# Attention scores of a hybrid decoder: the low-part query product over all 128 rows, and the causal mask added in the bias

## The chip, the cores and the metric

One Trainium2 chip, one of its cores. The metric is the device time of one launch in microseconds (us); lower is better. Five engines work side by side: TensorE (PE, with its weight loads PEld), VectorE (DVE), ScalarE (ACT), GpSimd (POOL) and SyncE (SP), whose queue issues nearly all DMAs. Each engine executes its own instructions in the order in which the program lists them and waits at each for the semaphores that it needs.

## The reference

A trunk of two layers on 1024 tokens of 1024 channels, all in float32. Layer 0 is a gated convolution (Conformer) with a feed-forward network and an embedding gate; layer 1 is forgetting attention with 16 heads of 64 channels, again with a feed-forward network and a gate. The part that matters here:

```
q = (hn @ w_q).reshape(B, S, N_HEADS, HEAD_DIM) * (HEAD_DIM ** -0.5)
...
s = jnp.einsum("bqhd,bkhd->bhqk", q_blk, k,
bias = c_blk[:, :, :, None] - c_bhs[:, :, None, :]
causal = k_pos[None, :] <= q_pos[:, None]
s = jnp.where(causal, s + bias, NEG_BIG)
pr = jax.nn.softmax(s, axis=-1)
return jnp.einsum("bhqk,bkhd->bqhd", pr.astype(v.dtype), v)
```

`c` is the running sum of the log forget gates, one number per head and token.

## The kernel before, in words

**Split operands.** TensorE multiplies float32r operands, so each float32 operand is kept as two parts, a high one `h` (a cast, `split`, L107) and a low one `l` (the subtraction, L108); a product is three products of parts (`mm3`, L130). Weights come panel by panel (`panel`, L110): a DMA from SP (L113) into a tile `raw` (L112, two buffers in the whole program, tag "raw"), the norm's gain multiplied in on GpSimd (L118), then the split. Squares and their sum for a norm's statistics are in `rstd` (squares L166, sum `acc` L187 and L189, its own buffer).

**Attention** (`attention`, L458) goes over 8 pairs of heads. A pair has 8 units: 4 groups of 256 queries (u = 3, 2, 1, 0; in the last pair 0, 1, 2, 3) times two heads (e = 0, 1), 64 units in all. `scores` (L683) makes a unit's probabilities for two blocks of 128 queries: GpSimd writes the bias c(query) - c(key) into a slot of the tile `pr` (L696), TensorE adds up the score in pieces of up to 512 keys, DVE adds bias and score and takes the row's extreme (L714), ACT exponentiates and sums (L720), DVE inverts the sum (L721), GpSimd scales (L722). A score piece is two products: L705 over 128 rows (the high query part times both key parts) and L706 over the 64 rows of this head (the low query part `ql` times the high key part). In the last piece of a block a third product adds the causal mask: a bf16 identity times a bf16 mask of 128 columns (L710). There are 192 pieces, 3 per unit on average, and 128 blocks. `values` (L725) transposes the probabilities on TensorE (L770), splits them, and multiplies by V (L740); it runs one unit behind `scores`.

**Fills.** Between the units stand products that do not depend on them: the queries and keys of the next pair (`project_qk`, psq and psk), the values of the next four heads (`project_v`, psv). In the last two pairs, when there is nothing left to project, the output product (`out_product`, L558, ps_wo) of the first five pairs stands there; its weights come through `panel` too. A scheduler puts the program in order by its own estimates; the pools of tiles and their numbers of buffers enter into it. Every tile that is not yet released makes the engine that wants it wait.

Of the kernel before, what the change touches and what calls it, by code (L numbers as in the profile page):

```python
# [10 lines left out]
F32 = mybir.dt.float32  # L11
F32R = mybir.dt.float32r
BF16 = mybir.dt.bfloat16
# [5 lines left out]
P = 128  # L19
# [15 lines left out]
# columns of the packed per-channel vectors: name -> (offset, number of 128-row tiles)  # L35
# [24 lines left out]
class K:  # L60
    def __init__(self, ctx, tc, a):
# [3 lines left out]
        self.wp = ctx.enter_context(tc.tile_pool(name="wp", bufs=3))  # L65
# [13 lines left out]
        # the sigmoid's table holds what the first stage needs  # L79
# [9 lines left out]

    def slot(self, shape, dt, name):  # L90
        return self.big.tile(shape, dt, name=name, tag="big")

    def tmp(self, name, dt=F32, cols=HB):
        return self.tp.tile([P, cols], dt, name=name, tag="t")
# [15 lines left out]
    def panel(self, src, kt, name, gain=None, k0=0, width=P, sub=None):  # L110
        nc = self.nc
        raw = self.wp.tile([P, kt * width], F32, name=f"raw_{name}", tag="raw", bufs=2)  # L112
# [31 lines left out]
    def bcast(self, col, name):  # L144
        """[128 tokens, 4] -> PSUM [128, 512]: the tokens' value in every partition."""
# [25 lines left out]
    def rstd(self, xs, name, late=0, ahead=URGENT):  # L171
        """xs(k) -> [128, 512]; 1/sqrt(mean of squares + eps): SBUF [128 tokens, 4], PSUM [128, 512]."""
# [4 lines left out]
        def reduce(x, first, last):  # L177
            # the sum over the partitions, one token per partition
# [7 lines left out]
        acc = self.tp.tile([P, HB], F32, name=f"acc_{name}", tag="acc", bufs=1)  # L186
# [25 lines left out]
    def operand(self, hT, h, gain, name, pool=None):  # L212
        """float32r parts of h * gain; the norm's factor per token is applied to the products."""
# [31 lines left out]
    def ple_proj(self, l, ahead):  # L245
        """p[l] @ w_proj[l], transposed, kept in DRAM."""
# [3 lines left out]
        for k in range(KP):  # L250
            with self.tc.high_priority(offset=ahead()):
                raw = self.wp.tile([P, T], F32, name=f"raw_p{l}{k}", tag="raw", bufs=2)
# [17 lines left out]
    def glu(self, hT, u, cs, halves, x, s):  # L270
        """first pointwise product and gate, into u [128, 30 + T] per channel tile."""
# [46 lines left out]
            # two sums in PSUM, so that a step reads SBUF once and leaves GpSimd its port  # L318
# [13 lines left out]
    def ln_silu(self, y, h):  # L332
        nc = self.nc
        yk = lambda k: y[:, k, :]
        acc = self.tp.tile([P, HB], F32, name=f"acc_m{h}", tag="acc", bufs=1)
# [80 lines left out]
    def first(self, hT):  # L416
        """convolution layer, first FFN and embedding gate."""
        nc, tc = self.nc, self.tc
        self.subs = (nc.gpsimd, None)
        with ExitStack() as c1:  # L420
            self.psum_pools(c1, 0, 4)
# [36 lines left out]
    def attention(self, hT):  # L458
# [6 lines left out]
        with ExitStack() as c2:  # L465
            self.at = self.pool(c2, "at", 2)
# [6 lines left out]
            mask = self.cp.tile([P, P], BF16, name="mask")  # L473
# [5 lines left out]
            idb = self.cp.tile([P, P], BF16, name="idb")  # L479
            nc.vector.tensor_copy(idb, self.ident)  # L480
            self.mask, self.idb = mask, idb
# [53 lines left out]
        c3 = ExitStack()  # L535
        self.psum_pools(c3, 2)
# [11 lines left out]
    def load_o(self, od, p):  # L548
        """head pair p of the output product's operand."""
        if self.xo is None:  # L550
            self.xo = [self.xpair("xo", h) for h in range(NH)]
        raw = self.wp.tile([P, T], F32, name=f"raw_o{p}", tag="raw", bufs=2)
# [5 lines left out]
    def out_product(self, k0, k1, halves=(0, 1)):  # L558
# [10 lines left out]
    def gates(self, cd):  # L569
        """cumulative log forget gates: DRAM [head, token] and SBUF [token, block, head]."""  # L570
        nc = self.nc
        g = self.at.tile([P, 2, T], F32, name="gate", tag="pr")
        u, e, lt, x = (g[:, 0, i * P : (i + 1) * P] for i in range(4))
        z = self.zf.rearrange("p b n -> p (b n)")
        # log_sigmoid(z) = min(z, 0) - log1p(exp(-|z|)), log1p with its rounding put back
# [11 lines left out]
        # sums within a block of 128 tokens, and over the blocks before it  # L587
# [10 lines left out]
        rows = g[0:N, 1, :]  # L598
        for h in range(NH):
# [3 lines left out]
            nc.scalar.copy(rows[:, h * HB : (h + 1) * HB], st[0:N, :])  # L603
# [12 lines left out]
    def project_v(self, g, dst):  # L616
        """values of the four heads of group g, in pieces."""
# [31 lines left out]
    def project_qk(self, p, dst):  # L649
        """queries and keys of the two heads of pair p, in pieces."""  # L650
# [217 lines left out]
```

## Time and profile before

| | us |
|---|---|
| device time, median of 3 runs | 2696.07 (2693.39 to 2699.38) |
| span of the profiled execution (first to last instruction) | 2692.4 |
| PE busy | 2628.9 |
| DVE / ACT / POOL busy | 1532.9 / 1003.4 / 592.8 |

The profiled execution has no time of its own on the page beside its span; the median of the runs lies 3.7 us above that span. Within the span the first layer ends near 1190 us, attention goes from there to 1859 us, and the second layer's feed-forward network, gate and last norm take the rest. A PE instruction's "busy" time is longer than its distance to the next one, since matmuls overlap; the distance from start to start is what a product costs in a row of products.

### The profile page before, as it was taken

To read this page: it belongs to the slowest core of one execution; us is meant where nothing else is said; L and a number is where in the kernel's file an instruction comes from. 1 tells how busy PE (TensorE), PEld (TensorE's weight loads), DVE (VectorE), ACT (ScalarE), POOL (GpSimd) and SP (SyncE) were. 2 spreads that over 40 slices of the span, in tenths; PEclk is the share of its full clock that TensorE was granted. 3 is DMA by queue.
4 is the path that set the end of the run, shared out by engine and by line. 5 is a ranking of instruction groups with operands and counts; after the bars stand their busy time and mean duration, and the time that the engine had idled before them with its cause. 6 is when DMAs were issued, how large, how long until landed. Compare 5 with 4: busy or idle time off the path is not lost.

```text
span 2692.4 us, 31503 instructions
## 1 busy us (share of the span) xinstructions
PE 2628.9 (98%) x12184; PEld 2110.3 (78%) x12184; DVE 1532.9 (57%) x2536; ACT 1003.4 (37%) x1608; POOL 592.8 (22%) x525
## 2 busy tenths in 40 slices
PE   7997999999999999999999999999999999999998
PEld 6885778888888888888777787778888888888886
DVE  7999999734444335566666666766323323223466
ACT  5245433333333224334555554654312202113242
POOL 3464544444000000013444443340000000000000
PEclk9998999999999999999999999999999999999998
DMA  3124222222222222231111111321111111111123
GB/s 128 47 73 170 68 89 94 93 95 93 96 87 94 94 94 98 94 123 56 57 39 54 40 56 62 102 83 62 47 47 48 47 47 48 47 47 51 48 98 133
DMA packets 63973, 205.26 MB, mean 76 GB/s; under 512 B 7360, under 2 KB 12096, under 8 KB 63312
## 3 DMA queue, kind: packets, MB, share of 16 engines
q1 hardware_dynamic: 62672, 199.06, 21.9%
q10 hardware_dynamic: 1152, 4.19, 0.4%
q8 instruction: 96, 1.57, 0.2%
q14 instruction: 53, 0.43, 0.1%
HBM read 182.71 MB, written 20.51 MB: 75 GB/s over the span
## 4 chain that ended last, share of the span: by engine, by line
PE 89%; DVE 6%; issue 2%; POOL 1%; ACT 1%; DMA 1%; POOLq 0%; DVEq 0%; SPq 0%; ACTq 0%
PE ps_fb L130 27%; PE ps_fa L130 25%; PE ps_gt L130 5%; PE psv L130 4%; PE psk L130 3%; PE psq L130 3%; PE ps_wo L130 3%; PE pg L130 3%; PE pa L130 3%; PE po L740 3%; PE s L706 3%; DVE ya L324 2%; PE t L770 2%; PE ps_pw L130 2%; PE s L705 1%
## 5 line engine op out<-in xcount | busy, mean ns | idle before, releaser
L324 DVE SCALAR_TENSOR_TENSOR ya<-u,wdw,ya 128x512 f32<-128x512 f32 x420 | 284.8, 748 | 0.0
L107 ACT CAST wh_fb<-raw_fb 128x1024 fp32r<-128x1024 f32 x96 | 100.6, 1051 | 429.2 <-PE ps_fb L130 306.9
L376 DVE SCALAR_TENSOR_TENSOR fa<-ps_fa,bs_f 128x512 f32<-128x512 f32 x128 | 87.8, 690 | 272.0 <-PE ps_fa L130 269.2
L197 POOL TENSOR_TENSOR r_g<-ms_g,mhalf 128x4 f32<-128x4 f32 x4 | 5.3, 1322 | 1071.3 <-DVE ms_g L195 1071.3
L107 ACT CAST wh_fa<-raw_fa 128x1024 fp32r<-128x1024 f32 x96 | 100.8, 1050 | 348.1 <-PE ps_fa L130 166.8
L130 PE MATMUL ps_fa<-f10xh,wl_fa 128*128 128x512 f32 x512 | 202.7, 396 | 0.0
L130 PE MATMUL ps_fa<-f10xl,wh_fa 128*128 128x512 f32 x512 | 202.5, 396 | 0.0
L130 PE MATMUL ps_fa<-f10xh,wh_fa 128*128 128x512 f32 x512 | 202.5, 396 | 0.0
L382 DVE TENSOR_TENSOR hTb<-ps_fb,hTb 128x512 f32<-128x512 f32 x64 | 44.3, 692 | 246.1 <-PE ps_fb L130 246.1
L108 DVE TENSOR_TENSOR pt<-t,pt 128x512 fp32r<-128x512 f32 (+1 forms) x160 | 99.8, 634 | 90.2 <-ACT pt L107 89.8
L382 DVE TENSOR_TENSOR hT<-ps_fb,hT 128x512 f32<-128x512 f32 x64 | 44.0, 690 | 172.0 <-PE ps_fb L130 171.9
L378 ACT ACTIVATE fa<-fa 128x512 f32<-128x512 f32 x128 | 80.4, 630 | 156.2 <-DVE fa L376 156.1
L722 POOL TENSOR_SCALAR pr<-pr,sm 128x896 f32<-128x896 f32 (+7 forms) x128 | 98.0, 768 | 165.3 <-DVE sm L721 164.2
L107 ACT CAST pt<-t 128x512 fp32r<-128x512 f32 (+1 forms) x160 | 85.1, 542 | 125.6 <-PE t L770 115.7
L714 DVE CUSTOM_DVE_ANT_0 pr<-s,pr 128x512 f32<-128x512 f32 (+2 forms) x192 | 103.2, 552 | 47.9 <-POOL pr L696 20.2
L696 POOL TENSOR_SCALAR pr<-cb,ctok 128x896 f32<-128x896 f32 (+7 forms) x128 | 101.0, 796 | 94.2 <-PE t L770 64.0
L720 ACT ACTIVATE pr<-pr,sm 128x896 f32<-128x896 f32 (+7 forms) x128 | 99.3, 776 | 57.4 <-DVE sm L719 37.3
L740 PE MATMUL po<-pt,V 128*128 128x256 f32 x640 | 115.6, 301 | 1.9 <-ACT pt L107 1.9
L130 PEld LDWEIGHTS ps_fa<-f10xl,wh_fa 128*128 128x128 f32 x512 | 96.3, 188 | 23.1
L130 PEld LDWEIGHTS ps_fa<-f10xh,wl_fa 128*128 128x128 f32 x512 | 96.3, 188 | 23.1
L130 PEld LDWEIGHTS ps_fa<-f10xh,wh_fa 128*128 128x128 f32 x512 | 96.3, 188 | 23.1
L108 POOL TENSOR_TENSOR wl_fa<-raw_fa,wh_fa 128x1024 fp32r<-128x1024 f32 x32 | 80.1, 2504 | 96.8 <-ACT wh_fa L107 96.8
(357 smaller groups left out, 7431.4 us busy)
## 6 DMA issues: line engine op xcount, KB each, us to landing
raw_fa<-in_wf SPq DMA_DIRECT2D x96, 512.0 KB, 3.3
raw_fb<-in_wf SPq DMA_DIRECT2D x96, 512.0 KB, 3.3
raw_gt<-in_wgate SPq DMA_DIRECT2D x24, 512.0 KB, 3.4
proj<-pj SPq DMA_DIRECT2D x32, 256.0 KB, 2.4
raw_pw<-in_wpw SPq DMA_DIRECT2D x16, 512.0 KB, 3.4
lpj<-proj SPq DMA_DIRECT2D x32, 256.0 KB, 3.3
cb<-cd SPq DMA_DIRECT2D x16, 512.0 KB, 3.9
raw_wo<-in_wo SPq DMA_DIRECT2D x16, 320.0 KB, 2.8
```

The lines of the kernel that those rows point to most:

```text
L107: copy(h, src)
L108: sub.tensor_tensor(l, src, h.bitcast(F32), ALU.subtract)
L130: self.nc.tensor.matmul(ps, p[:, k, :], q[:, k, :], start=(start and k == k0 and n == 0), stop=(stop and k == kt - 1 and n == 2),)
L324: nc.vector.scalar_tensor_tensor(d, s(j), w(j), o, ALU.mult, ALU.add)
L376: nc.vector.scalar_tensor_tensor(t, ps, 0.0, s[h][1], ALU.max, ALU.mult)
L382: nc.vector.tensor_tensor(hT[h][:, j, :], ps, hT[h][:, j, :], ALU.add)
L696: nc.gpsimd.tensor_scalar(z, cb[:, 0:W], -1.0, self.ctok[:, i, n : n + 1], ALU.mult, ALU.add)
L706: nc.tensor.matmul(ps[:, 0:cols], ql[r, q], qk[r, 2 + e, kk], start=False, stop=not last)
L714: nc.vector.tensor_tensor_reduce(zz, ps[:, 0 : hi - lo], zz, -1.0, 3.0e38, ALU.add, ALU.min, sm[:, m : m + 1])
L720: nc.scalar.activation(z, z, AF.Exp, bias=sm[:, 0:1], scale=-1.0, accum_out=sm[:, 2:3])
L722: nc.gpsimd.tensor_scalar(z, z, sm[:, 3:4], 1.0, ALU.mult, ALU.mult)
L740: nc.tensor.matmul(po, V[:, j, n % 4, :], pt[:, q, c : c + 256], start=(j == 0 and q == 0), stop=(jp == u and jj == 1 and q == 1),)
```

## The change

The low query part goes into one of two fixed tiles with a plane for each head; the other head's 64 rows are zero, written once (four GpSimd memsets of 64x1024). The low product then runs over 128 rows with the same key operand as L705. The mask product is gone; GpSimd adds a float32 mask of 128x128 to the last 128 columns of each block's bias. The rows of `c` go to DRAM with their sign turned, so that the bias is one addition. `pr` is split into two tags of its own sizes. The tiles that this needs come out of the working pools, which now belong to a stage each: in attention `raw` has 1 buffer (before 2) and the ring of `tmp` has 3 (before 4), the statistics' `acc` comes from that ring, and the output product's panels in attention use the slots of `cb` (the broadcast rows of c, two buffers).

```diff
+    def work_pools(self, ctx, n, raw=2, t=4):
+        self.wp, self.raws = self.pool(ctx, f"wp{n}", 3), raw
+        self.tt = self.pool(ctx, f"tt{n}", t)
...
-        raw = self.wp.tile([P, kt * width], F32, name=f"raw_{name}", tag="raw", bufs=2)
+        if pool is None:
+            raw = self.wp.tile([P, kt * width], F32, name=f"raw_{name}", tag="raw", bufs=self.raws)
+        else:
+            raw = pool.tile([P, kt * width], F32, name=f"raw_{name}", tag=tag)
...
-        acc = self.tp.tile([P, HB], F32, name=f"acc_{name}", tag="acc", bufs=1)
+        acc = self.tmp(f"acc_{name}")
...
+            self.work_pools(c2, 1, 1, 3)
             self.at = self.pool(c2, "at", 2)
...
+            self.qls = [self.at.tile([P, 2, T], F32R, name=f"ql{i}", tag=f"ql{i}", bufs=1) for i in range(2)]
+            for ql in self.qls:
+                for e in range(2):
+                    nc.gpsimd.memset(ql[(1 - e) * HD : (2 - e) * HD, e, :].bitcast(F32), 0.0)
...
-                for _ in self.out_product(0, KSPLIT, (h,)):
+                for _ in self.out_product(0, KSPLIT, (h,), self.at):
...
-            w = self.panel(self.a["wo"][j][:, k0 * P : k1 * P], k1 - k0, f"wo{k0}{j}{halves[0]}")
+            w = self.panel(self.a["wo"][j][:, k0 * P : k1 * P], k1 - k0, f"wo{k0}{j}{halves[0]}", pool=pool, tag="cb")
...
-            nc.scalar.copy(rows[:, h * HB : (h + 1) * HB], st[0:N, :])
+            nc.scalar.mul(rows[:, h * HB : (h + 1) * HB], st[0:N, :], -1.0)
...
-        pr = self.at.tile([P, 2, T], F32, name=f"pr{n}{u}", tag="pr")
+        pr = [self.at.tile([P, T - (1 - b) * P], F32, name=f"pr{n}{u}{b}", tag=f"pr{b}") for b in range(2)]
...
-            nc.gpsimd.tensor_scalar(z, cb[:, 0:W], -1.0, self.ctok[:, i, n : n + 1], ALU.mult, ALU.add)
+            nc.gpsimd.tensor_scalar(z, cb[:, 0:W], self.ctok[:, i, n : n + 1], None, ALU.add)
+            nc.gpsimd.tensor_tensor(z[:, W - P : W], z[:, W - P : W], self.mask, ALU.add)
...
-                    ps[:, 0:cols], ql[r, q], qk[r, 2 + e, kk], start=False, stop=not last
-                )
-                if last:
-                    nc.tensor.matmul(
-                        ps[:, W - P - lo : W - lo], self.idb, self.mask, start=False, stop=True
-                    )
+                    ps[:, 0:cols], ql[:, e, q], qk[:, 2 + e, kk], start=False, stop=True
+                )
```

Line numbers of the changed kernel differ: bias L709, mask addition L710, products L718 and L719, scaling L731, output product's panels L120, memsets of `ql` L493.

**The order, SP, from the end of the embedding gate into attention, before.** lpj are the gate's loads (256 KB each), raw_wv the three panels of the first values' weights, raw_q and raw_k the first query and key panels, hd the store of the residual (2 MB each).

```order
L394 DMA lpj_7871<-proj_1600 128x512
L113 DMA raw_wv_8269<-in_wv 128x816
L394 DMA lpj_7903<-proj_1600 128x512
L394 DMA lpj_7941<-proj_1600 128x512
L113 DMA raw_wv_8276<-in_wv 128x816
L394 DMA lpj_7973<-proj_1600 128x512
L394 DMA lpj_8011<-proj_1600 128x512
L113 DMA raw_wv_8283<-in_wv 128x544
L394 DMA lpj_8043<-proj_1600 128x512
L394 DMA lpj_8081<-proj_1600 128x512
L113 DMA raw_q_8554<-in_wq 128x1024
L394 DMA lpj_8113<-proj_1600 128x512
```

The same queue in the changed kernel:

```order
L401 DMA lpj_8084<-proj_1603 128x512
L401 DMA lpj_8116<-proj_1603 128x512
L120 DMA raw_wv_8284<-in_wv 128x816
L470 DMA hd<-hT_87 128x4096
L470 DMA hd<-hT_92 128x4096
L120 DMA raw_wv_8291<-in_wv 128x816
L120 DMA raw_wv_8298<-in_wv 128x544
L120 DMA raw_q_8569<-in_wq 128x1024
L120 DMA raw_k_8642<-in_wk 128x1024
```

All three panels moved behind the gate's last load, and two of them behind the two stores; each panel from the second on waits until DVE has split the one before it out of the single buffer. On DVE the split of the second panel now stands behind all 14 additions of the statistics' sums.

**The order, PE, the first output product, before** (t and po are transposes and value products of a unit, s its scores):

```order
L770 MATMUL t_13542<-ident,pr_13389 128x128 x3
L705 MATMUL s_13637<-qk_12586 128x512
L706 MATMUL s_13637<-qk_12586,ql_12587 128x512
L710 LDWEIGHTS idb
L710 MATMUL s_13637<-mask,idb 128x128
L130 MATMUL ps_wo_14381<-xoh_13614,wh_wo_14377 128x512
L130 MATMUL ps_wo_14381<-xol_13615,wh_wo_14377 128x512
```

and in the changed kernel:

```order
L749 MATMUL po_14290<-pt_14283,V_11777 128x256 x3
L718 MATMUL s_14300<-qk_13282 128x512
L719 MATMUL s_14300<-qk_13282,ql_8160 128x512
L137 MATMUL ps_wo_14453<-xoh_13674,wh_wo_14449 128x512
L137 MATMUL ps_wo_14453<-xol_13675,wh_wo_14449 128x512
```

Before, 509 of the 640 value products stand ahead of the first output product, now 608; in both kernels 480 stand ahead of the last projection psk. The first panel's slot is that of the `cb` of the last pair, free after the bias of the last unit but one. The mask products are gone between L705/L706 and what follows.

**The order, POOL, the first units in the changed kernel** (before, the four biases, one panel's multiplication and four scalings in a row, no additions):

```order
L709 TENSOR_SCALAR pr_8715<-cb_8711,ctok 128x896
L709 TENSOR_SCALAR pr_8716<-cb_8711,ctok 128x1024
L709 TENSOR_SCALAR pr_8816<-cb_8713,ctok 128x896
L709 TENSOR_SCALAR pr_8817<-cb_8713,ctok 128x1024
L125 TENSOR_TENSOR raw_q_9273<-raw_q_9273,vec 128x1024
L710 TENSOR_TENSOR pr_8715<-pr_8715,mask 128x128
L710 TENSOR_TENSOR pr_8716<-pr_8716,mask 128x128
L710 TENSOR_TENSOR pr_8816<-pr_8816,mask 128x128
L710 TENSOR_TENSOR pr_8817<-pr_8817,mask 128x128
L731 TENSOR_SCALAR pr_8715<-pr_8715,sm_8719 128x896
L731 TENSOR_SCALAR pr_8716<-pr_8716,sm_8734 128x1024
L125 TENSOR_TENSOR raw_k_9447<-raw_k_9447,vec 128x1024
```

A panel's multiplication now stands ahead of the mask additions and another between the scalings; what waits for its DMA there holds back what is behind it.

## Rows read from the trace of the kernel before

**Rows 1.** The page, part 1 (busy time, share) and part 4 (the chain).
```profile
PE 2628.9 (98%) x12184; PEld 2110.3 (78%) x12184; DVE 1532.9 (57%) x2536; ACT 1003.4 (37%) x1608; POOL 592.8 (22%) x525
...
PE 89%; DVE 6%; issue 2%; POOL 1%; ACT 1%; DMA 1%; POOLq 0%; DVEq 0%; SPq 0%; ACTq 0%
```

**Rows 2.** Busy time by stretch: PE, PEld, DVE, ACT, POOL, then PEclk, DMA share, GB/s.
```profile
1366.00:1507.00 141.00, 140.46 (x826) 110.96 (x825) 89.55 (x240) 78.45 (x162) 65.63 (x87) 1.00 0.13 46
...
1859.00:2579.00 720.00, 720.00 (x3104) 580.84 (x3103) 232.14 (x291) 166.57 (x229) 2.04 (x2) 1.00 0.14 48
```

**Rows 3.** Timeline of PE at 1397 us: start, length, line, product.
```profile
1397.41 0.28 PE L130 MATMUL psv<-wl_wv,atxh 128*128 128x256 f32 x1
1397.53 0.40 PE L705 MATMUL s<-qk 128*128 128x512 f32 x1
1397.86 0.49 PE L706 MATMUL s<-qk,ql 64*128 64x512 f32 x1
1398.28 0.23 PE L710 MATMUL s<-mask,idb 128*128 128x128 bf16 x1
1398.32 0.36 PE L130 MATMUL psv<-wh_wv,atxl 128*128 128x256 f32 x1
1398.52 0.40 PE L705 MATMUL s<-qk 128*128 128x512 f32 x1
1398.85 0.50 PE L706 MATMUL s<-qk,ql 64*128 64x512 f32 x1
1399.28 0.39 PE L130 MATMUL psv<-wh_wv,atxh 128*128 128x256 f32 x1
1399.51 0.28 PE L130 MATMUL psv<-wl_wv,atxh 128*128 128x256 f32 x1
```

**Rows 4.** PEld groups, 1225 to 1825 us: count | busy, mean ns | idle before.
```profile
L706 PEld LDWEIGHTS s<-qk,ql 64*128 64x128 f32 x192 | 35.4, 184 | 42.9 <-issue 36.1
```

**Rows 5.** Low product L706 up to 1699 us: ns min/median/max, first and last start.
```profile
L706 PE MATMUL s<-qk,ql x155: 379/491/502, 1245.4 to 1692.8; 64*128 64x512 f32 x80, 64*128 64x256 f32 x49, 64*128 64x384 f32 x26
```

**Rows 6.** Groups of POOL, whole program, shapes kept apart.
```profile
L316 POOL TENSOR_TENSOR y<-y,cm 128x512 f32<-128x512 f32 x30 | 42.0, 1400 | 5.2 <-ACT cm L314 3.5
...
L118 POOL TENSOR_TENSOR raw_q<-raw_q,vec 128x1024 f32<-128x1024 f32 x8 | 16.0, 1994 | 18.5 <-DMA raw_q<-in_wq 18.5
...
L696 POOL TENSOR_SCALAR pr<-cb,ctok 128x128 f32<-128x128 f32 x16 | 6.0, 372 | 3.6 <-PE t L770 2.7 <-POOL pt L772 0.4
```

**Rows 7.** The DMA queue of SP around the end of the embedding gate.
```profile
1167.06 0.33 SPq L113 DMA_DIRECT2D raw_wv<-in_wv  x1
...
1189.92 0.32 SPq L462 DMA_DIRECT2D hd<-hT  x1
...
1192.97 0.32 SPq L462 DMA_DIRECT2D hd<-hT  x1
```

**Rows 8.** The chain of waits from 1183 to 1260 us: start, length, what.
```profile
1189.44 5.78 PE psv L130 x44
...
1221.24 0.47 PE psq L130 x2
```

**Rows 9.** Timeline of DVE: the statistics' sums at 1199 us.
```profile
1199.74 3.99 DVE L189 TENSOR_TENSOR acc_at<-acc_at,sq_at 128x512 f32<-128x512 f32 x4
```

**Rows 10.** DMA issues by line: count, KB each, median us from issue to landing.
```profile
hd<-hT SPq DMA_DIRECT2D x2, 2048.0 KB, 9.1
...
raw_wv<-in_wv SPq DMA_DIRECT2D x2, 408.0 KB, 3.2
```

**Rows 11.** Last key product and all output products: count, ns, first and last start.
```profile
L130 PE MATMUL psk<-atxh,wl_k x128: 392/394/502, 1233.3 to 1698.7; 128*128 128x512 f32 x128
...
L130 PE MATMUL ps_wo<-xoh,wl_wo x128: 392/394/496, 1718.6 to 1858.5; 128*128 128x512 f32 x128
```

**Rows 12.** Busy time by stretch (columns as in rows 2), behind the last key product.
```profile
1707.00:1710.00 3.00, 1.80 (x14) 1.62 (x14) 2.90 (x7) 2.95 (x7) 2.19 (x2) 1.00 0.46 161
1710.00:1718.00 8.00, 7.57 (x27) 4.95 (x27) 7.33 (x21) 4.87 (x10) 2.47 (x4) 0.61 0.32 107
```

More of the change, by code (lines that the diff above doesn't have):

```diff
@@ L64, in __init__ @@
         self.cp = ctx.enter_context(tc.tile_pool(name="cp", bufs=1))
-        self.wp = ctx.enter_context(tc.tile_pool(name="wp", bufs=3))
         self.tp = ctx.enter_context(tc.tile_pool(name="tp", bufs=4))
@@ L93, in tmp @@
     def tmp(self, name, dt=F32, cols=HB):
-        return self.tp.tile([P, cols], dt, name=name, tag="t")
+        return self.tt.tile([P, cols], dt, name=name, tag="t")
     def psum_pools(self, ctx, n, mm=6):
@@ L108, in split, with panel @@
         sub.tensor_tensor(l, src, h.bitcast(F32), ALU.subtract)
-    def panel(self, src, kt, name, gain=None, k0=0, width=P, sub=None):
+    def panel(self, src, kt, name, gain=None, k0=0, width=P, sub=None, pool=None, tag=None):
         nc = self.nc
-        raw = self.wp.tile([P, kt * width], F32, name=f"raw_{name}", tag="raw", bufs=2)
+        if pool is None:
+            raw = self.wp.tile([P, kt * width], F32, name=f"raw_{name}", tag="raw", bufs=self.raws)
+        else:
+            raw = pool.tile([P, kt * width], F32, name=f"raw_{name}", tag=tag)
         nc.sync.dma_start(raw, src)
@@ L251, in ple_proj @@
             with self.tc.high_priority(offset=ahead()):
-                raw = self.wp.tile([P, T], F32, name=f"raw_p{l}{k}", tag="raw", bufs=2)
+                raw = self.wp.tile([P, T], F32, name=f"raw_p{l}{k}", tag="raw", bufs=self.raws)
                 nc.sync.dma_start(raw, self.a["pT"][l, :, k * T : (k + 1) * T])
@@ L334, in ln_silu @@
         yk = lambda k: y[:, k, :]
-        acc = self.tp.tile([P, HB], F32, name=f"acc_m{h}", tag="acc", bufs=1)
+        acc = self.tmp(f"acc_m{h}")
         nc.vector.tensor_tensor(acc, yk(0), yk(1), ALU.add)
@@ L420, in first @@
         with ExitStack() as c1:
+            self.work_pools(c1, 0)
             self.psum_pools(c1, 0, 4)
@@ L472, in attention @@
             self.sqp, self.sqt = self.at, "pt"
-            mask = self.cp.tile([P, P], BF16, name="mask")
+            mask = self.cp.tile([P, P], F32, name="mask")
             nc.gpsimd.memset(mask, 0.0)
@@ L478, in attention @@
             )
-            idb = self.cp.tile([P, P], BF16, name="idb")
-            nc.vector.tensor_copy(idb, self.ident)
-            self.mask, self.idb = mask, idb
+            self.mask = mask
+            self.qls = [self.at.tile([P, 2, T], F32R, name=f"ql{i}", tag=f"ql{i}", bufs=1) for i in range(2)]
+            for ql in self.qls:
+                for e in range(2):
+                    nc.gpsimd.memset(ql[(1 - e) * HD : (2 - e) * HD, e, :].bitcast(F32), 0.0)
             self.tri = self.cp.tile([P, P], F32, name="tri")
@@ L535, in attention @@
         c3 = ExitStack()
+        self.work_pools(c3, 2)
         self.psum_pools(c3, 2)
@@ L551, in load_o @@
             self.xo = [self.xpair("xo", h) for h in range(NH)]
-        raw = self.wp.tile([P, T], F32, name=f"raw_o{p}", tag="raw", bufs=2)
+        raw = self.wp.tile([P, T], F32, name=f"raw_o{p}", tag="raw", bufs=self.raws)
         self.nc.sync.dma_start(raw, od[p])
@@ L556, in load_o, with out_product @@
             self.split(raw[:, h * HB : (h + 1) * HB], x[0][:, p, :], x[1][:, p, :])
-    def out_product(self, k0, k1, halves=(0, 1)):
+    def out_product(self, k0, k1, halves=(0, 1), pool=None):
         hn, xo = self.hn, self.xo
         for j in range(KT):
-            w = self.panel(self.a["wo"][j][:, k0 * P : k1 * P], k1 - k0, f"wo{k0}{j}{halves[0]}")
+            w = self.panel(self.a["wo"][j][:, k0 * P : k1 * P], k1 - k0, f"wo{k0}{j}{halves[0]}", pool=pool, tag="cb")
             for h in halves:
@@ L571, in gates @@
         nc = self.nc
-        g = self.at.tile([P, 2, T], F32, name="gate", tag="pr")
-        u, e, lt, x = (g[:, 0, i * P : (i + 1) * P] for i in range(4))
+        g = self.at.tile([P, T - P], F32, name="gate0", tag="pr0")
+        gr = self.at.tile([P, T], F32, name="gate1", tag="pr1")
+        u, e, lt, x = (g[:, i * P : (i + 1) * P] for i in range(4))
         z = self.zf.rearrange("p b n -> p (b n)")
@@ L597, in gates @@
         nc.vector.tensor_copy(ctok.rearrange("p b n -> p (b n)"), st[:, 0:P])
-        rows = g[0:N, 1, :]
+        rows = gr[0:N, :]
         for h in range(NH):
@@ L654, in project_qk @@
         qk = self.slot([P, 4, T], F32R, f"qk{p}")
-        ql = self.at.tile([P, T], F32R, name=f"ql{p}", tag="ql")
+        ql = self.qls[p % 2]
         dst[p] = (qk, ql)
@@ L666, in project_qk @@
                     nc.scalar.copy(qk[r2, e, c], t[r])
-                nc.vector.tensor_tensor(ql[r, c], t[r], qk[r, e, c].bitcast(F32), ALU.subtract)
+                nc.vector.tensor_tensor(ql[r, e, c], t[r], qk[r, e, c].bitcast(F32), ALU.subtract)
             yield
@@ L688, in scores @@
         cb = cur[p, "cb"][e]
-        r = slice(e * HD, (e + 1) * HD)
-        pr = self.at.tile([P, 2, T], F32, name=f"pr{n}{u}", tag="pr")
+        pr = [self.at.tile([P, T - (1 - b) * P], F32, name=f"pr{n}{u}{b}", tag=f"pr{b}") for b in range(2)]
         for b in range(2):
@@ L694, in scores @@
             q = slice(i * P, W)
-            z = pr[:, b, 0:W]
-            nc.gpsimd.tensor_scalar(z, cb[:, 0:W], -1.0, self.ctok[:, i, n : n + 1], ALU.mult, ALU.add)
+            z = pr[b][:, 0:W]
+            nc.gpsimd.tensor_scalar(z, cb[:, 0:W], self.ctok[:, i, n : n + 1], None, ALU.add)
+            nc.gpsimd.tensor_tensor(z[:, W - P : W], z[:, W - P : W], self.mask, ALU.add)
             sm = self.tp.tile([P, 8], F32, name=f"sm{n}{i}", tag="sm", bufs=6)
@@ L701, in scores @@
                 cols = max(hi - lo, 256)
-                last = hi == W
                 ps = self.sp.tile([P, HB], F32, name=f"s{n}{i}{lo}", tag="s")
@@ L769, in values @@
                     j = 2 * jp + jj
-                    nc.tensor.transpose(ps[:, c : c + P], pr[:, b, j * P : (j + 1) * P], self.ident)
+                    nc.tensor.transpose(ps[:, c : c + P], pr[b][:, j * P : (j + 1) * P], self.ident)
             if f:
```

## The prediction, made before the changed kernel ran

> **What bounds the kernel now.** I read the page first. PE is busy for 98% of the span and holds 89% of the chain of waits [rows 1]: what shortens PE's row of products shortens the kernel, as long as PE has products to go on with. The stretches say how full that row is. In the feed-forward network 3104 products take 720 us [rows 2], 0.232 us for each of 512 columns. A projection of 256 columns is followed 0.12 us later by the next product (1397.41 to 1397.53) [rows 3]. In the middle of attention 16 units take 141 us, 8.8 us a unit, and in that stretch the others are far from full: DVE 89.55 us (5.6 a unit), ACT 78.45 (4.9), POOL 65.63 (4.1) [rows 2]. So PE bounds these units.
>
> Then the timeline, at the score products [rows 3]. L705 starts at 1397.53 and L706 at 1397.86: 0.33 where 512 columns need 0.232, so 0.10 lost. From L706 to the next product it is 0.42 (1397.86 to 1398.28) and 0.43 (1398.85 to 1399.28): 0.19 lost. The product behind takes 0.23 (1399.28 to 1399.51) instead of 0.12: 0.11 lost. With a mask, 0.04 for the mask (1398.28 to 1398.32) and 0.20 instead of 0.12 behind it: 0.12. Either way a score piece costs PE about **0.40 us** beyond its columns. The reader is to see that nothing is waited for: the weight load of L706 comes with idle time put down to "issue", 36.1 us over 192 loads, 0.19 each [rows 4]. L706 is the only product here of the form 64*128, all its neighbours are 128*128. I read it as PE emptying itself at each change of form, once in and once out.
>
> That rests on the forms of the rows; the Trainium skill, "TensorEngine Tiling (Array Packing)", section "Key Properties", says the same, that a change of tiling mode drains TensorE. It gives no length, so the trace's 0.40 us is the only price.
>
> **The change, part by part.**
>
> *Low product over 128 rows, no mask product.* The columns stay, so the product itself costs what its neighbour costs. 155 of the 192 pieces are issued up to 1699 us, when psk ends and PE runs short of fills [rows 5, 11]. 155 x 0.42 = **-65 us**; I take 0.42, since a few pieces with 256 columns and a mask lose slightly more than the rows shown. Ends: 0.35 (only the two changes around L706: 0.10 + 0.19, with 0.06 of the rest) gives -54, 0.47 gives -73. The other 37 are in the tail below.
>
> *Mask additions.* 128 additions of 128x128 with two operands. None is in the trace. A one-operand bias of that size takes 0.37 us, a two-operand one of 512 columns 1.40 [rows 6]; I take 0.6, nearer the row with the same 128 columns, so 1.2 us a unit. POOL goes from 4.1 to 5.3 us a unit, against PE's new 8.8 - 3 x 0.42 = 7.5: hidden while fills last. Even at 1.40 POOL has 6.9, still under 7.5. The add stands between bias and reduction and lengthens a unit's own way, and `raw` has one buffer: I allow **+5 us** (0 to 20) of small stalls over the 48 units of pairs 0 to 5. The four memsets and the sign cost nothing: POOL waits at that time anyway.
>
> *From the gate into attention.* The three panels of the first values were loaded during the gate; the last was issued at 1167.06 [rows 7]. psv starts at 1189.44 and psq follows at 1221.24 [rows 8]. Now panel 1 needs panel 0's split, then a DMA that shares the channel with two stores of 2 MB, issued until 1192.97 and 9.1 us in landing [rows 7, 10], the multiplication, and on DVE the 14 additions, of which four took 3.99 us when paced by ACT's squares [rows 9]. From 1193 on that is 9 (at 0.65 each) to 14 us, and I put panel 1 at 1209. Panel 2 follows one cycle of the single buffer later: 3.2 us landing [rows 10], about 2 us multiplication and about as much for the split, less for a panel of two thirds the size: 1215. Behind it PE still has 6 of the 8 value products, 6 x 24 x 0.13 = 19 us (44 took 5.78 [rows 8]), and less than 1 us of two others: end at 1234 instead of 1221, and some 2 us at a low clock. **+15 us** (8 to 20).
>
> *The first units.* raw_q and raw_k of the next pairs come one buffer cycle of 7 to 8 us after another, and POOL's and DVE's rows hold them between mask additions, scalings and splits. Behind each of three such waits stand the next additions and the split of the transposes, for which PE waits. Fills cover part: **+6 us** (0 to 12).
>
> *The last two pairs.* From 1699 to 1859 PE does 16 units and all 384 output products, three times 128 [rows 11]. 384 x 0.232 = 89 us, so 71 us are the units', 4.4 each: PE is well filled. Now the first output product stands behind 608 of 640 value products instead of 509, since its panel waits for the slot of `cb`. 128 value products, 14 units, run with no fill, and what bounds a unit then is DVE and the way from bias to transposes. I price a unit at DVE's present 5.6 us [rows 2], less 8 us since the first two units' scores are done by then: 70 us. The last two units overlap output products at about 5 us of PE each: 10. Then 89. Sum 169 against 160: +9, in which the 37 cheaper pieces are contained. To that a colder clock: when PE had been busy only 1.80 of 3 us, the granted clock of the next 8 us averaged 0.61, so between the levels of 1.2 and 2.4 GHz [rows 12]; 8 x 0.39 = 3 us were lost there. A row of such gaps makes it **+14 us** in all (ends: 4.4 us a unit throughout -8; the PE-bound 7.5 us with no gain from the missing fills, 14 x 7.5 + 99 - 160 = +44, cut to +40 by the work done ahead).
>
> On that clock the Trainium skill, "TensorE: Matmul & The Clock Gate", section "HAM oscillation — how this bites in real kernels", says that a loop whose work is shorter than its waits falls back to the low clock in each turn. The rows agree with one fall behind one gap. If all 14 units ran at half clock, their own 3.4 us of PE (8.8 less fills and 1.3) would be 6.8, over DVE's 5.6, and the tail +31 instead of +14: that is part of the second rival.
>
> *The second layer and stage 0* keep their order but for a few rows: 0 (-3 to +3).
>
> **Sum.** -65 + 5 + 15 + 6 + 14 = -25. On the profiled span 2692.4 that is 2667; the median of the runs stands 3.7 us above that span, so **2671 us**, 0.9% less.
>
> **The rivals.**
>
> 1. *The covers hold.* Transition +8, first units 0, loop 0, tail -8, gain 65 to 73: -65 to -73, about **2627 us**. For it: PE's busy share near 1 all along attention, and DVE at 5.6 against 7.5 us. Against: the output product's place in PE's order, which is written down. Chance 0.17.
> 2. *Gain eaten at both ends.* Tail +31 to +40 with the clock falling in every unit, transition 20, first units and loop 12 to 20: -2 to +15 with the gain of 65, so **2694 to 2711 us**. For it: 14 units without fill are certain by the order. Against: DVE's own share per unit is lower for u = 0 and 1. Chance 0.13.
> 3. *Slower: POOL held back by the single raw buffer through the whole loop.* 20 panels (7 q, 7 k, 6 wv) are multiplied on POOL in line with bias, mask and scaling. Each waits for its DMA, which waits for the split of the one before. If PE loses t us at each, the gain of 65 is gone, with the 15 and 14 of the ends, at t = 36 / 20 = 1.8 us. At 3.5 us it is -65 + 70 + 29 = +34: **2730 us**. For it: POOL already waits 18.5 us for 8 raw_q [rows 6], with two buffers. Against: a cycle of 8 us for 3 panels in 8 units of 7.5 us leaves room. Chance 0.08.
> 4. *The change doesn't do what it says.* The gaps belong to the second product on the same PSUM tile, not to the form, and stay. Only the masks' 128 x 0.12 = 15 us go, the ends cost 35 to 50: **2720 us**. Against: the 0.19 stands behind L706 and only 0.10 behind L705. Chance 0.04.
>
> **How the numbers follow.** The forecast's case has 0.58, from 2640 to 2692. The measurement of this kernel tells 0.2%, 5.4 us, from no change. Faster: all of 1 and nearly all of the forecast: 0.17 + 0.56 = 0.73. Within 0.2%: the forecast's end and the lower part of 2: 0.02 + 0.08 = 0.10. Slower: the rest of 2, and 3 and 4: 0.05 + 0.08 + 0.04 = 0.17. The range leaves out the larger part of case 1 (some 0.08), 3 and 4: **2630 to 2705**.
>
> **What would show it.** No row of the form 64*128; the distance behind a low product equal to 0.23 for 512 columns; 16 units in the middle in 120 us instead of 141. psq starts near 1234 after the shift of what stands ahead; PE idle near 1200 with DVE's split of the second panel as its releaser. From the last psk to the first ps_wo some 70 us with PE waiting for DVE and a granted clock under 1. Mask additions near 0.6 us. The prediction is wrong if the middle does not shrink (3, 4), if POOL's idle time ahead of raw_q grows by tens of us and PE waits for POOL (3), or if the tail from the last psk to the last ps_wo takes less than 155 or more than 195 us (1, 2).

## The result, and the profile after

The changed kernel takes **2720.81 us** (median of 4 runs, 2720.02 to 2726.07) against 2695.86 for the kernel before: a ratio of **1.0095, 95% interval 1.008 to 1.0109**. It is slower by 0.95%; forecast were 2671 us and a range of 2630 to 2705. The profiled execution is the slowest of the four: 2726.07 us, with a span of 2724.3.

The first table cuts both spans at the same products: the last product of layer 0's gate (ps_gt), the first query product (psq), the last key product (psk), the last output product (ps_wo), the last product of layer 1's gate, the end. The columns f1 to g1 are experiments from below.

| us | before | changed | difference | f1 | f2 | f3 | g1 |
|---|---|---|---|---|---|---|---|
| start to last ps_gt, layer 0 | 1187.3 | 1168.7 | -18.6 | 1169.2 | 1159.5 | 1168.9 | 1159.5 |
| to first psq | 33.8 | 47.8 | +14.0 | 47.6 | 32.4 | 47.6 | 47.5 |
| to last psk | 477.6 | 494.1 | +16.5 | 433.7 | 475.9 | 433.6 | 434.1 |
| to last ps_wo | 159.8 | 192.0 | +32.2 | 168.1 | 158.2 | 158.8 | 159.2 |
| to last ps_gt, layer 1 | 815.4 | 790.7 | -24.7 | 790.8 | 792.5 | 790.7 | 792.7 |
| to the end | 18.5 | 31.0 | +12.5 | 31.0 | 18.5 | 31.0 | 18.6 |
| span | 2692.4 | 2724.3 | +31.9 | 2640.4 | 2637.0 | 2630.6 | 2611.6 |

The page of the changed kernel, parts 1 and 4:

```profile
PE 2565.2 (94%) x12056; PEld 2133.0 (78%) x12056; DVE 1548.7 (57%) x2535; ACT 1005.9 (37%) x1608; POOL 780.1 (29%) x657
...
PE 78%; DVE 10%; POOL 4%; issue 3%; ACT 2%; DMA 2%; POOLq 0%; DVEq 0%; SPq 0%; ACTq 0%
```

PE does 64 us less work than in [rows 1] and yet the kernel is slower: PE's share of the chain fell from 89 to 78%, and POOL has 187 us more. The 128 mask additions explain a third of that. The groups of POOL in attention, shapes kept apart, show the rest:

```profile
L710 POOL TENSOR_TENSOR pr<-pr,mask 128x128 f32<-128x128 f32 x128 | 64.1, 512 | 0.0
L709 POOL TENSOR_SCALAR pr<-cb,ctok 128x1024 f32<-128x1024 f32 x16 | 45.6, 2850 | 0.0
...
L731 POOL TENSOR_SCALAR pr<-pr,sm 128x1024 f32<-128x1024 f32 x16 | 18.9, 1181 | 25.8 <-DVE sm L730 19.9 <-DVE sm L728 5.6
```

The scaling takes 1.18 us for 1024 columns, as before. The bias, the same kind of instruction over the same columns, takes **2.85 us**; before it took 1.19 (f2 below has the row). All biases together went from 101 us to 223.5.

What the change meant to do on PE, it does. The timeline of PE at a score product, to be held against [rows 3]:

```profile
1396.84 0.39 PE L718 MATMUL s<-qk 128*128 128x512 f32 x1
1397.07 0.40 PE L719 MATMUL s<-qk,ql 128*128 128x512 f32 x1
1397.31 0.28 PE L137 MATMUL psv<-wh_wv,atxl 128*128 128x256 f32 x1
```

0.23 and 0.24 us from start to start where it was 0.33 and 0.43: the time lost around the low product is gone.

The way through attention, from the first query product to the last key product and then to the first output product (PE, PEld, DVE, ACT, POOL busy, then PE's granted clock):

```profile
1217.00:1711.00 494.00, 447.00 (x2572) 380.12 (x2572) 312.33 (x777) 258.26 (x513) 356.85 (x368) 0.96 0.14 50
```

```profile
1711.00:1805.00 94.00, 66.24 (x317) 50.41 (x317) 61.41 (x173) 50.65 (x117) 75.59 (x91) 0.78 0.21 77
```

The same stretch of the kernel before, from its first query product to its last key product:

```profile
1221.00:1699.00 478.00, 475.44 (x2690) 372.60 (x2690) 302.14 (x783) 259.07 (x518) 208.24 (x268) 1.00 0.15 52
```

In the first stretch PE is idle for 47 of 494 us, where it was idle for 3 of 478, and its clock, 1.00 before, is 0.96 on the mean; in the second it is 0.78. No single wait is long: the two largest of PE's own in the first stretch (us in total, times, longest) are

```profile
PE t L779 <- POOL pr L731: 9.5, 11, 2.5
PE s L718 <- DVE sm L723: 9.3, 15, 1.6
```

And one thing nothing in the change speaks of: the feed-forward network of layer 1 is faster, 3105 products in 700 us against 3104 in 720 [rows 2].

```profile
1903.00:2603.00 700.00, 700.00 (x3105) 580.15 (x3104) 233.71 (x295) 168.22 (x233) 2.42 (x2) 1.00 0.14 49
```

In an unbroken row the distance from product to product is 0.227 us now and 0.233 before, in every stage of the program.

### The profile page after: what moved, and what is told of

Same layout as the page of the kernel before. It is cut to its first block, busy times and chain, and to the rows that moved or that the text cites. A ratio compares the mean times of both kernels' runs of the same rounds, so it can differ in the third digit from the quotient of the medians.

```text
span 2724.3 us, 31354 instructions
## 1 busy us (share of the span) xinstructions
PE 2565.2 (94%) x12056; PEld 2133.0 (78%) x12056; DVE 1548.7 (57%) x2535; ACT 1005.9 (37%) x1608; POOL 780.1 (29%) x657
## 4 chain that ended last, share of the span: by engine, by line
PE 78%; DVE 10%; POOL 4%; issue 3%; ACT 2%; DMA 2%; POOLq 0%; DVEq 0%; SPq 0%; ACTq 0%
PE ps_fb L137 25%; PE ps_fa L137 24%; PE ps_gt L137 6%; PE ps_wo L137 3%; DVE ya L331 3%; PE pg L137 3%; PE pa L137 3%; PE psv L137 3%; PE psq L137 2%; PE psk L137 2%; POOL pr L709 2%; PE ps_pw L137 2%; PE t L779 1%; PE po L749 1%; DVE pr L723 1%
## 5 line engine op out<-in xcount | busy, mean ns | idle before, releaser
L709 POOL TENSOR_SCALAR pr<-cb,ctok 128x896 f32<-128x896 f32 (+7 forms) x128 | 223.5, 1755 | 33.8 <-PE t L779 29.2
L749 PE MATMUL po<-pt,V 128*128 128x256 f32 x640 | 127.7, 317 | 19.5 <-ACT pt L111 8.5
L731 POOL TENSOR_SCALAR pr<-pr,sm 128x896 f32<-128x896 f32 (+7 forms) x128 | 101.6, 799 | 90.7 <-DVE sm L730 77.3
L779 PE MATMUL t<-ident,pr 128*128 128x128 f32 x576 | 103.6, 298 | 24.6 <-POOL pr L731 13.5
L749 PEld LDWEIGHTS po<-pt,V 128*128 128x128 f32 x640 | 98.6, 205 | 34.8 <-ACT pt L111 14.5
L723 DVE CUSTOM_DVE_ANT_0 pr<-s,pr 128x512 f32<-128x512 f32 (+3 forms) x192 | 104.0, 552 | 36.4 <-POOL pr L710 14.8
```

The source lines that it names most:

```text
L709: nc.gpsimd.tensor_scalar(z, cb[:, 0:W], self.ctok[:, i, n : n + 1], None, ALU.add)
L723: nc.vector.tensor_tensor_reduce(zz, ps[:, 0 : hi - lo], zz, -1.0, 3.0e38, ALU.add, ALU.min, sm[:, m : m + 1])
L731: nc.gpsimd.tensor_scalar(z, z, sm[:, 3:4], 1.0, ALU.mult, ALU.mult)
L749: nc.tensor.matmul(po, V[:, j, n % 4, :], pt[:, q, c : c + 256], start=(j == 0 and q == 0), stop=(jp == u and jj == 1 and q == 1),)
L779: nc.tensor.transpose(ps[:, c : c + P], pr[b][:, j * P : (j + 1) * P], self.ident)
```

## The experiments

These theories came out of this. The bias's operation is the cost (A), or the mask additions and the single raw buffer are (B). The product rate depends on where operands lie in SBUF (C). The remaining differences have causes of their own: the late output product (D), the norms' running sum in the ring of tmp (E), and the panels' way from the gate into attention (F).

**e1_bias_two_ops**: the changed kernel with

```diff
-            nc.gpsimd.tensor_scalar(z, cb[:, 0:W], self.ctok[:, i, n : n + 1], None, ALU.add)
+            nc.gpsimd.tensor_scalar(z, cb[:, 0:W], self.ctok[:, i, n : n + 1], 0.0, ALU.add, ALU.add)
```

> The changed kernel with one edit: the bias on GpSimd again has two operations (add the token's c, then add 0.0) instead of one. Theory A (the one-operation form of this instruction is what went wrong: 1.76 us on average where the old form took 0.80, so POOL binds the units): bias back to about 0.8 us on average, POOL's busy time from 780 to about 660 us, and the time 2640 to 2675 us, so 45 to 80 us under the changed kernel. Theory B (the mask addition ahead of each reduction and the single raw buffer hold the units back, and the longer bias only fills POOL's waits): POOL's busy time falls as well, the time stays within 10 us of 2721.

Measured: 2789.16 us, 68 us slower than the changed kernel. The guess at the number of operations was wrong, and the way it was wrong is the clue. Its bias group on POOL:

```profile
L709 POOL TENSOR_SCALAR pr<-cb,ctok 128x1024 f32<-128x1024 f32 x16 | 59.3, 3706 | 0.0
```

Two additions take 3.71 us, one 2.85, a product and an addition 1.19, the scaling's two products 1.18: that points to the kind of the first operation and not to their number, which f1 tests. The time followed POOL's durations up, which speaks for A's place.

**e2_before_again**: the kernel before, no edit.

> The kernel before, unchanged, for a profile beside the others on the same chip. In the profile of before a 512-column product follows the next by 0.233 us, in that of the changed kernel by 0.227, in every stage. If it is the chip or the run, this profile shows 0.227 and a span near 2660 to 2692; if it is the program, 0.233 and a span near 2692. Time near 2696 either way by the runs so far.

Measured: 2695.9 us, span 2693.9, 430 products in 800 to 900 us as in the first profile of before, 443 in the changed kernel. The rate belongs to the program.

**e3_before_one_op**: the kernel before with

```diff
-            nc.gpsimd.tensor_scalar(z, cb[:, 0:W], -1.0, self.ctok[:, i, n : n + 1], ALU.mult, ALU.add)
+            nc.gpsimd.tensor_scalar(z, cb[:, 0:W], self.ctok[:, i, n : n + 1], None, ALU.add)
...
-            nc.scalar.copy(rows[:, h * HB : (h + 1) * HB], st[0:N, :])
+            nc.scalar.mul(rows[:, h * HB : (h + 1) * HB], st[0:N, :], -1.0)
```

> The kernel before with the bias alone changed to one operation (rows of c stored with the sign turned). Theory A: bias 1.76 us on average, POOL's busy time from 593 to about 715 us; POOL then has about 6.1 us a unit against PE's 8.8, so it lies beside PE in the middle and lengthens only each unit's own way: 0 to 25 us slower. Theory B: bias durations unchanged or the time unchanged, 2696 within 5 us.

Measured: 2751.92 us, ratio 1.0195 (1.0178 to 1.0212): +54 us, twice the upper end expected, from this one edit (the scheduler's order moves a little with it). The stretch from the first psq to the last psk grew from 478 to 520 us:

```profile
1222.00:1742.00 520.00, 501.38 (x2691) 388.79 (x2689) 308.74 (x781) 261.56 (x519) 307.09 (x268) 0.96 0.14 47
```

POOL is busy for 307 of 520 us, far from full. PE is idle for 19 of them instead of 3, and its busy time for the same number of products grew from 475 to 501 us: 16 and 26, the 42 us. At a mean clock of 0.96 some 0.04 x 520 = 21 of these are the clock's. A longer step on a unit's own way makes many small gaps, and behind some of the gaps the clock falls. From 1387 to 1397 us PE was idle for 2 of 10 us; in the next ten it was busy throughout, at a clock of 0.55:

```profile
1397.00:1407.00 10.00, 10.00 (x42) 8.02 (x43) 4.64 (x19) 4.61 (x14) 4.63 (x10) 0.55 0.30 105
```

In the ten us after that it is back at 1.00. The Trainium skill, "TensorE: Matmul & The Clock Gate", section "A second HAM failure mode: psum-queue depth-cycling", tells of another kernel in which short idle times between groups of products make the clock go up and down. These rows agree.

**e4_mask_by_product**: e1 with the mask by the old bf16 product instead of L710.

> The kernel of e1_bias_two_ops with the mask again by a bf16 product instead of GpSimd's additions (low product still over 128 rows, pools as in the change). Theory A: POOL loses about 64 us that were beside other work, PE gains 128 products of 0.06 to 0.12 us: 5 us faster to 12 us slower than e1. Theory B: the additions were the hold-up, 30 us or more faster than e1.

Measured: 2750.2 us, 39 us faster than e1, as B wanted. But with a bias of 3.71 us POOL is busy for 404 of the 542 us from psq to psk in e1, and 61 us taken off it may show there whatever they were. f4 repeats it with a fast bias.

**f1_bias_mult_add**: the changed kernel with

```diff
-            nc.gpsimd.tensor_scalar(z, cb[:, 0:W], self.ctok[:, i, n : n + 1], None, ALU.add)
+            nc.gpsimd.tensor_scalar(z, cb[:, 0:W], 1.0, self.ctok[:, i, n : n + 1], ALU.mult, ALU.add)
```

> The changed kernel with the bias as a product by 1.0 and then the addition of the token's c, the order of operations that the kernel before had. Theory A2 (what is slow on GpSimd is this instruction when its first operation is an addition: 2.85 us for 1024 columns with one, 3.71 with two additions, 1.19 with a product and an addition): 1024 columns in 1.2 us, bias 0.8 us on average, POOL's busy time near 655 us, and the units bound by PE again: 2625 to 2665 us. Theory B (mask addition and single raw buffer): 2700 us or more, since they stay.

Measured: **2641.48 us**, ratio to before 0.9792 (0.9776 to 0.9809), 79 us under the changed kernel by one edited line (here too the scheduler's order moves: 597 value products stand ahead of the first output product instead of 608). POOL's busy time is 661.3 us; the group and the stretch from psq to psk:

```profile
L709 POOL TENSOR_SCALAR pr<-cb,ctok 128x1024 f32<-128x1024 f32 x16 | 19.8, 1239 | 0.0
```

```profile
1217.00:1650.00 433.00, 419.08 (x2597) 368.48 (x2596) 315.23 (x783) 258.05 (x518) 263.43 (x371) 1.00 0.17 57
```

The clock is back at 1.00 and PE idles for 14 us instead of 47. Mask additions and the single raw buffer are still there, and the kernel is fast: A holds in its second form, and B alone doesn't make it slow. The scaling (L731) also takes the scalar of each partition first, in a product, and is fast, so that scalar's place isn't the cause. Whether a single product, or an addition followed by a product, is fast wasn't run.

**f2_before_aligned**: the kernel before with two unused tiles of 64 bytes a partition

```diff
+        nc.vector.memset(self.cp.tile([P, 16], F32, name="padc"), 0.0)
         self.wp = ctx.enter_context(tc.tile_pool(name="wp", bufs=3))
         self.tp = ctx.enter_context(tc.tile_pool(name="tp", bufs=4))
+        nc.vector.memset(self.tp.tile([P, 16], F32, name="padt", tag="padt", bufs=1), 0.0)
```

> The kernel before with two unused tiles of 64 bytes a partition, which move the pool of the weight panels from an address of 64 modulo 128 to one of 0, as it is in the changed kernel, and leave the big operands at 0. Theory C (the 512-column products of the changed kernel follow each other at 0.227 instead of 0.233 us because of where the weights lie in SBUF): 0.227 us in every stage and about 2655 to 2668 us, some 30 to 40 us faster than before. Rival: the rate belongs to something else in the program, 0.233 us and 2697 us within 5.

Measured: **2639.49 us**, ratio 0.9789 (0.9774 to 0.9803): 59 us from 128 bytes of nothing (the kernel before took 2698.25 beside it), more than expected, since some 9100 of the 512-column products in the whole program follow one of their kind without a gap and each gains 6 ns (55 us; the spans differ by 55.4). Its bias, for the row promised above:

```profile
L698 POOL TENSOR_SCALAR pr<-cb,ctok 128x1024 f32<-128x1024 f32 x16 | 19.0, 1190 | 0.0
```

**f3_wo_in_raw**: f1 with

```diff
-                for _ in self.out_product(0, KSPLIT, (h,), self.at):
+                for _ in self.out_product(0, KSPLIT, (h,)):
```

> The kernel of f1_bias_mult_add with the output product's panels of the attention stage in the raw buffer instead of the slots of cb, so that they need not wait for the last pair's bias. Theory D (the tail is lengthened by the late first output product, as predicted, 14 us): 5 to 25 us faster than f1, psk to the last output product near 160 us. Rival: one raw buffer feeds the output product too slowly, and it is no faster or slower than f1.

Measured: 2634.28 us, 7.2 us faster than f1; the last psk to the last ps_wo takes 158.8 instead of 168.1 us (table), and the first ps_wo follows the last psk after 30 instead of 72 us. D holds, with a smaller size.

**f4_mask_by_product**: f1 with the mask by the bf16 product.

> The kernel of f1_bias_mult_add with the mask by a bf16 product on TensorE instead of the additions on GpSimd. If the additions are hidden beside PE, as predicted: PE's 128 products cost 5 to 15 us more than f1. If the additions lengthen each unit's way or bind POOL: 5 to 20 us faster than f1.

Measured: 2642.6 us (2641.77 to 2646.0), which overlaps with f1's 2640.04 to 2642.45. POOL loses 59 us (602.3 busy), the stretch from psq to psk grows from 433.7 to 437.1 us, the tail to the last ps_wo shrinks from 168.1 to 164.1. Neither expectation came: with a fast bias the mask costs about the same on either engine, 7 us of busy PE in this stretch (425.8 against 419.1) or 3 us more of idle PE (13.9 against 11.2). That the additions are hidden altogether isn't shown. The run also settles the fourth rival: the mask's product follows the low product on the same PSUM tile after 0.23 us (1382.18 to 1382.41, 512 columns) where it was 0.42 [rows 3], so the gap went with the 64 rows and not with a second product on the tile.

**g1_own_acc**: f3 with the statistics' sum in its own buffer in the first and third stage

```diff
         self.tt = self.pool(ctx, f"tt{n}", t)
+        self.ac = None if n == 1 else self.pool(ctx, f"ac{n}", 1)
...
-        acc = self.tmp(f"acc_{name}")
+        acc = self.acc(name)
```

> The kernel of f3_wo_in_raw with the statistics' running sum again in a buffer of its own in the first and third stage (in attention it stays in the ring of tmp). Theory E (taking that sum from the ring delays the last norm, which in the changed kernel ends 31 us behind the last gate product instead of 18.5, and the first stage by some 9 us): end of the span 18 to 20 us behind the last gate product again, the embedding gate of layer 0 ends near 1160 instead of 1169 us, 15 to 22 us faster than f3, about 2615 us. Rival: these belong to the pools' new places or other buffers, and it stays at 2634.

Measured: **2613.75 us**, ratio to before 0.9692 (0.9678 to 0.9707), 20.5 us faster than f3 and the fastest of all. The gate of layer 0 ends at 1159.5, the span 18.6 us behind the last gate product. In the changed kernel the timeline of DVE shows what came late there: thirteen of the last norm's sums start behind the last gate product (2693.3), ten of them in these two rows,

```profile
2697.45 5.27 DVE L196 TENSOR_TENSOR acc_fin<-acc_fin,sq_fin 128x512 f32<-128x512 f32 x7
...
2702.82 2.28 DVE L196 TENSOR_TENSOR acc_fin<-acc_fin,sq_fin 128x512 f32<-128x512 f32 x3
```

while in the kernel before the last sum starts at 2672.26, ahead of the last gate product (2673.9), and of the norm only the statistic itself and the final scaling are left:

```profile
2679.86 0.16 DVE L195 TENSOR_SCALAR ms_fin<-st_fin 128x4 f32<-128x4 f32 x1 [2.75 <-PE st_fin L181]
2683.27 5.36 DVE L410 SCALAR_TENSOR_TENSOR hTb<-hTb,vec,bc_fin 128x512 f32<-128x512 f32 x8 [3.25 <-PE bc_fin L150]
```

**g2_before_weights_0_rest_64, g3_change_weights_64, h1_before_both_64**: g2 is f2 without its second tile; g3 is f3 with 64 bytes ahead of each stage's weight pool and 64 behind it; h1 is f2 without its first tile.

> The kernel before with one unused tile of 64 bytes a partition ahead of the weight panels only: the weights come to an address of 0 modulo 128, the big operands that stream through (and the stage pools) to 64. Theory C1 (the weights' address alone sets the rate): 0.227 us from product to product, near 2640 us. Theory C2 (the streamed operand's address counts as well): 0.233 us or more, 2690 us or more.

> The kernel of f3_wo_in_raw with the weight panels of each stage moved by 64 bytes to an address of 64 modulo 128, as they were before the change, everything else at 0. Theory C: 0.233 us again from product to product and 45 to 65 us slower than f3, 2680 to 2700 us. Rival (the rate had another source in the old kernel): within 5 us of f3.

> The kernel before with one unused tile of 64 bytes ahead of the big operands only, so that the weight panels and the streamed operands both lie at 64 modulo 128. Theory C2 (each of the two has to lie at 0): 0.233 us from product to product or more, near 2697 us. Theory C3 (they have to lie alike): 0.227 us, near 2640 us.

The stretch from 2100 to 2200 us, where PE is in the feed-forward network throughout, of f2, g2, g3 and h1 in this order (the figure in the first brackets counts the products):

```profile
2100.00:2200.00 100.00, 100.00 (x443) 82.84 (x442) 25.52 (x30) 13.33 (x16) 0.00 (x0) 1.00 0.14 48
```

```profile
2100.00:2200.00 100.00, 100.00 (x431) 80.55 (x430) 28.23 (x34) 17.88 (x23) 0.00 (x0) 1.00 0.14 48
```

```profile
2100.00:2200.00 100.00, 100.00 (x431) 80.66 (x430) 24.83 (x29) 11.88 (x13) 0.00 (x0) 1.00 0.13 47
```

```profile
2100.00:2200.00 100.00, 100.00 (x443) 82.84 (x442) 26.41 (x32) 14.43 (x17) 0.00 (x0) 1.00 0.14 48
```

The addresses in this table are worked out from the sizes of the tiles in the kernels; no trace shows them.

| addresses modulo 128: weights, streamed operand | kernel | products in 2100 to 2200 us | time |
|---|---|---|---|
| 64, 0 | before | 431 | 2696 |
| 64, 0 | g3 (f3 with 0, 0: 2634.28) | 431 | 2680.04 |
| 0, 64 | g2 | 431 | 2698.48 |
| 0, 0 | f2 | 443 | 2639.49 |
| 0, 0 | the changed kernel | 442 | 2720.81 |
| 64, 64 | h1 | 443 | 2638.55 |

The rate is the better one when the two lie alike modulo 128, not when one of them lies at 0: C3. It is their distance that counts, 0 or 64 bytes; why it counts no run shows. It costs the old kernel 59 us, and moving only the weights by 64 bytes costs f3 46.

**g4_wv_panels_in_cb**: g1 with the first values' three panels in the idle slots of cb.

> The kernel of g1_own_acc with the three weight panels of the first values in the two slots of cb, which are idle then, instead of the single raw buffer. Theory F (the way from the gate into attention is 15 us longer because each panel waits for the split of the one before): from the last gate product to the first query product 36 to 42 us instead of 47.8, and 5 to 12 us faster than g1. Rival: the panels still come behind the gate's last loads and the two stores of 2 MB, and nothing is gained.

Measured: 2617.48 us, 3.7 us slower than g1; from the last gate product to the first psq 50.6 us instead of 47.5. The rival holds: in this order all three panels stand behind the two stores of hd. That the wait for the split of the panel before is the cause of the 15 us isn't shown by it; only that two more buffers alone don't cure it.

## Why the prediction was wrong

Forecast was 25 us less, measured 25 more. The account below is in spans; the profiled execution of the changed kernel is the slowest of its four, by 5 us.

| cause | forecast | shown by | us |
|---|---|---|---|
| bias with an addition as its first operation | 0 | changed less f1 | +84 |
| addresses of weights and streamed operands | 0 | f2 less before | -55 |
| statistics' sum taken from the ring of tmp | 0 (-3 to +3) | f3 less g1 | +19 |
| from the gate into attention | +15 | 47.6 less 32.4, f1 and f2 | +15 |
| psq to psk: products, loop, first units | -65 + 5 + 6 = -54 | 433.7 less 475.9, f1 and f2 | -42 |
| last two pairs | +14 | 168.1 less 158.2, f1 and f2 | +10 |

The sum is +31 where the spans differ by 31.9. The last three rows are the terms that the prediction had: -17 together where it said -25. f1, 2641.48 us, lies in the forecast range, but by the addresses, which no term held; that is luck.

- **The step that failed** is the sentence "The four memsets and the sign cost nothing". With the sign went the bias's operation, from a product and an addition to an addition alone, and I took fewer operations to be no dearer. (The Trainium skill, "GPSIMD Engine Reference", section "4.1 Engine selection", calls one-input work on GpSimd roughly line-rate; f1's 1.24 us for 1024 columns goes with that, the 2.85 us do not.) The only one-operand rows at hand had a product first (bias and scaling). The instruction became 2.2 times as long on the mean (1755 against 796 ns), 122 us more on POOL, of which 84 showed. The prediction bounded the mask addition, which the trace didn't show either, from the nearest rows; it gave the bias's edit no row and no bounds. The same edit cost the old kernel 54 us (e3): the rest comes with what else the change put in, and the mask additions are likely, worth 39 us beside a slow bias (e4) and nothing beside a fast one (f4). At 2.85 us that wasn't run.
- **POOL's margin** was argued from the shares: 5.3 us a unit against PE's 7.5. With the slow bias POOL's share is 357 of 494 us, still not full, and e3 lost 42 us in the same stretch with POOL at 307 of 520. A unit's own way counts before an engine is full: a unit with 1024 keys has two biases, 2.85 + 2.53 us in a row ahead of DVE's reductions, and PE's small gaps also cost it clock.
- **The gap around the low product** was read rightly and is gone. The term came out smaller, -42 instead of -54, though the stalls were as forecast: PE idles for 14 us in f1 and 3 in f2, 11 more where +5 and +6 were said. What was too large is the gain: PE's busy time in this stretch fell by 54 us (473.5 to 419.1) and not by 65. That is about 0.35 us for each of the 155 pieces, the prediction's lower end, and not 0.42.

```profile
1192.00:1668.00 476.00, 473.45 (x2688) 373.54 (x2688) 303.51 (x783) 258.93 (x517) 209.56 (x268) 1.00 0.16 52
```

- **The way into attention** was right to a microsecond in its sum. The second panel was ready 21.0 us behind the last gate product (split at 1188.70, 1.01 us long), against 1209 less 1187.3 = 21.7 in the working. That the old order of loads would cure it wasn't tried, and g4 shows that the single buffer isn't the whole cause.
- **The tail** was right in its place and in its stretch without fill, 72 us without a fill (f1) against 70 forecast, and f3 shows what it is worth: 9 us in spans, against 14. In the changed kernel the slow bias made it 94 us, at a mean clock of 0.78.
- **The second layer and stage 0** got "0 (-3 to +3)". Both ends were off: the sums in the ring made the first stage 9 us and the last norm 12 us longer, and the addresses gave 20 us or more in each half. The diff shows the first; I looked at its effect in attention only.
- **The rivals.** The third had the right sign, the right engine and nearly the time, 2730, by a wrong mechanism: f1 keeps the single raw buffer and is fast. The fourth falls by f4.

The fastest kernel is g1: the change with the product by 1.0, the output product's panels in raw, and the sum in its own buffer, 2613.75 us, 3.1% under the kernel before. Some 55 us of that are the addresses, which the old kernel could have had without any of it: held against f2 (2639.49), which has the addresses alone, f1 gains nothing and g1 26 us, 1.0%.

## What to carry to other kernels

When a diff rewrites an instruction "equivalently", price the new form like a new instruction: on GpSimd `a + s` and `a * 1.0 + s` are the same number at 2.85 and 1.24 us. When a change moves pools, list where the operands of the main loop lie in SBUF before and after, since a rate that changes in every stage has its cause there and not in the edit that one is looking at. And an engine at 60% of a stretch can still set its length, by the way from one unit's step to the next and by the clock that PE loses in the gaps.

## What the runs showed of the hardware

- GpSimd's tensor-scalar instruction on 128x1024 float32 with a scalar for each partition: product and addition 1.19 to 1.28 us over all runs, product and product 1.13 to 1.22, one addition 2.85 to 2.89, two additions 3.71. A two-operand addition of 128x128 took 0.51 on the mean, less than the 0.6 taken.
- A float32r product of 512 columns follows the one before after 0.227 us when weights and streamed operand start alike modulo 128 bytes in their partition (addresses worked out from the tiles' sizes), and after 0.233 when they differ by 64; four combinations, of two kernels. For the value projection's 256 columns, with the roles of panel and operand exchanged, it is 0.120 and 0.118: no gain there.
- From psq to psk the granted clock was 0.96 on the mean where PE idled for 19 us of 520 (e3) or 47 of 494 (the changed kernel, no wait over 2.5 us), and 1.00 where it idled for 14 of 433 (f1).
